# Summing the third and fourth kilocolumn of layer 0's modulation on VectorE during the gates and the merge, with a newly fitted order

## The chip, the cores and the metric

The kernel runs on one core of one Trainium2 chip. The metric is the time of one execution on the device in microseconds (us); shown is the median of several executions. The core's engines are TensorE (PE in the profile, with its weight loads as PEld), VectorE (DVE), ScalarE (ACT), GpSimd (POOL) and SyncE (SP), which issues nearly all DMAs here. Each engine runs its own instructions in the order in which the program lists them.

## What is computed

Two layers of a hybrid transformer over 256 latent and 256 context tokens of width 1024, all in float32. The part that the change touches is the modulation: a vector of 6144 numbers for each of the two conditioning vectors, six "kilocolumns" of 1024.

```python
s_c, s_cc = silu(c), silu(c_ctx)
for l in range(2):
    sh_m, sc_m, g_m, sh_f, sc_f, g_f = split(s_c @ w_mod[l] + b_mod[l], 6)         # latent tokens
    csh_m, csc_m, cg_m, csh_f, csc_f, cg_f = split(s_cc @ w_mod[l] + b_mod[l], 6)  # context tokens
    h = rmsnorm(x, norm_mix_g[l]) * (1 + sc_m) + sh_m
    y = merge(latent_attention(h), hyena(h), diff_attention(h))   # three branches, sigmoid gates, w_out
    x = x + g_m * y
    x = x + g_f * sqrelu_mlp(rmsnorm(x, norm_ffn_g[l]) * (1 + sc_f) + sh_f)
return rmsnorm(x, final_norm_g)
```

Kilocolumns 2 (`g_m`) and 3 (`sh_f`) of layer 0 are the "third and fourth". The first is needed at the residual that follows the output projection, the second at the norm before the feed-forward part.

## The kernel before

The work is a list of steps, `prog`, that the planner builds layer by layer (`layer`) and that the table `ORDER` permutes. `runner` walks through that list: it issues the weight loads on SyncE's queue as soon as a buffer of the ring is due, splits each weight piece ("unit") one unit ahead into a high part `whi` and a low part `wlo`, and calls the step. The table `CHOICE` says for single operations which engine takes them (A, D, P) or which PSUM bank ("m" is the bank `mod`). Below this the framework's scheduler sets the final order of each engine's instructions: it may pull a matmul forward into a place where it expects TensorE to wait.

A GEMM unit is 24 matmuls of 128x512 (lines 279, 280, 281: high times high, high times low and low times high over eight contraction tiles). Its weights come in a raw tile of 1 MB for two units, of which the ring holds two (`RAW_BUFS`); ScalarE makes `whi` (L231), VectorE or GpSimd `wlo` (L219), and there are three pairs of them (`UNIT_BUFS`).

Layer 0 runs in this order: input projections and latent attention (up to some 200 us), Hyena's long convolution and differential attention (to 300 us), gates and merge (300 to 451 us: 20 of the 24 gate units and eight branch steps), the output projection, then the feed-forward part (500 to 860 us). Layer 1 follows.

Layer 0's modulation is computed in two ways. Kilocolumns 0 and 1 are done at the start. Kilocolumns 2 to 5 are done on TensorE by `mod_group(0, 1)` and `mod_group(0, 2)`: eight steps each, and each step loads 1 MB of `w_mod` into the weight ring and issues four matmuls (L347) that write the four quarters of one PSUM bank. The weights are 32 columns wide (`spad`), so each matmul uses a quarter of the array's columns. A last step transposes the sums (L357) and adds the bias on VectorE. These 18 steps are woven into the attention steps.

Layer 1's modulation is done in another way, by `mod_cols`, during layer 0's feed-forward part: VectorE multiplies a loaded block `modr` by one number for each partition and adds it to one of two accumulators `macc` (L383; for the first block ScalarE does it, L381). When all eight blocks are in, four matmuls with a tile of ones sum over the partitions (`sums`, L397), and four transposes and two additions finish (`fin`, L406, L411).

Of the kernel before, what the change touches and what calls it, by code (L numbers as in the profile page):

```python
# [9 lines left out]
F32 = mybir.dt.float32  # L10
# [114 lines left out]
def backbone_kernel(ctx: ExitStack, tc: tile.TileContext, t, out):  # L125
# [5 lines left out]
    EG, TAIL, PT, PU, FD = (4, 14), 6, 4, 3, 2  # L131
    MQB, FB = 5, ("mod", "o")
# [34 lines left out]
    def bank2(tag, key):  # L167
        if "1" in key.split(".")[0][:2] and pick("bk" + tag + key, "-") == "m":
            return bank("mod", 1)
        return bank(tag)  # L170
# [198 lines left out]
    def mod_cols(l, c):  # L369
# [4 lines left out]
        def part(kt):  # L374
            def f(raw):
                if kt == 0:
                    box["acc"] = [S["ffn"].tile([128, 1024], F32, tag=f"macc{v}", name=f"macc{v}") for v in range(2)]
                for v, a in enumerate(box["acc"]):
                    sv = spad[:, kt, v:v + 1]
                    if kt == 0:  # L380
                        ACT.activation(out=a, in_=raw, func=AF.Copy, scale=sv)  # L381
                    else:
                        DVE.scalar_tensor_tensor(out=a, in0=raw, scalar=sv, in1=a, op0=ALU.mult, op1=ALU.add)  # L383
            return f
        for kt in range(KT):
            def load(kt=kt):
                raw = S["ffn"].tile([128, 1024], F32, tag="modr", name="modr", bufs=RAW_BUFS)
                SP.dma_start(out=raw, in_=t["w_mod"][l, kt * 128:(kt + 1) * 128, c * 1024:(c + 1) * 1024])
                return raw
            steps.append(Step(part(kt), blk=Blk(load, "ffn")))  # L390
# [1093 lines left out]
    def norm_into(l, w):  # L1484

        def f(s):
# [3 lines left out]
            if (l, w) == (DEPTH - 1, 1):  # L1490
                hb["r"] = t2k()[:, :NL]
                ACT.copy(hb["r"], r)
            make_h(l, w, s, r, own=True)
        return f

    def layer(l):
        nt = T if l == 0 else NL
        p = []
# [185 lines left out]
```

## Time and profile before

| | us |
|---|---|
| median of 3 runs (1324.16 to 1326.61) | 1326.32 |
| profiled execution, whole | 1327.46 |
| its span, first to last instruction | 1325.7 |
| TensorE busy | 1281.5 (97%) |
| VectorE busy | 868.3 (66%) |
| ScalarE busy | 579.7 (44%) |
| GpSimd busy | 262.9 (20%) |

Times in views of the trace count from the span's start. Matmuls are pipelined: a row shows a matmul as longer than the step to the next one, so what a matmul costs is read from start to start. In the timeline a row `x8` stands for eight records that follow each other; a float32 matmul leaves two records, so `x8` is four matmuls. The granted clock is 1.00 of 2.4 GHz in all stretches that matter here.

### The profile page before, as it was taken

To read this page: it belongs to the slowest core of one execution; us is meant where nothing else is said; L and a number is where in the kernel's file an instruction comes from. 1 tells how busy PE (TensorE), PEld (TensorE's weight loads), DVE (VectorE), ACT (ScalarE), POOL (GpSimd) and SP (SyncE) were. 2 spreads that over 40 slices of the span, in tenths; PEclk is the share of its full clock that TensorE was granted. 3 is DMA by queue.
4 is the path that set the end of the run, shared out by engine and by line. 5 is a ranking of instruction groups with operands and counts; after the bars stand their busy time and mean duration, and the time that the engine had idled before them with its cause. 6 is when DMAs were issued, how large, how long until landed. Compare 5 with 4: busy or idle time off the path is not lost. (4 is left out here: it accounts for less than half of the span.)

```text
span 1325.7 us, 19880 instructions
## 1 busy us (share of the span) xinstructions
PE 1281.5 (97%) x7934; PEld 1077.5 (81%) x7934; DVE 868.3 (66%) x1426; ACT 579.7 (44%) x1027; POOL 262.9 (20%) x233
## 2 busy tenths in 40 slices
PE   5999999999999999999999999998999999999997
PEld 3566777678888798787787877996788999999997
DVE  4776746865243568987584875588768557876555
ACT  4454552664222334332432331364546755645343
POOL 3111032210002112220100112122133343240210
PEclk8899999999999999999999999998999999999999
DMA  9643234443332324655563543332124355555552
GB/s 283 166 160 106 77 123 133 149 138 95 95 96 95 120 72 130 220 178 167 177 207 114 185 153 123 120 104 80 49 81 124 120 175 187 159 188 189 174 183 94
DMA packets 159790, 185.21 MB, mean 140 GB/s; under 512 B 4880, under 2 KB 149233, under 8 KB 157650
## 3 DMA queue, kind: packets, MB, share of 16 engines
q1 hardware_dynamic: 158162, 182.27, 43.7%
q0 software_dynamic: 928, 1.54, 0.4%
q8 instruction: 62, 1.02, 0.3%
q14 instruction: 30, 0.25, 0.1%
q10 hardware_dynamic: 608, 0.14, 0.0%
HBM read 182.88 MB, written 1.05 MB: 139 GB/s over the span
## 5 line engine op out<-in xcount | busy, mean ns | idle before, releaser
L231 ACT CAST whi<-raw 128x1024 fp32r<-128x1024 f32 x197 | 206.7, 1051 | 429.8 <-PE g L280 201.5
L279 PE MATMUL g<-hhi,whi 128*128 128x512 f32 (+2 forms) x1040 | 354.3, 341 | 4.3 <-DVE d L1179 1.7
L281 PE MATMUL g<-hhi,wlo 128*128 128x512 f32 (+2 forms) x1040 | 352.3, 339 | 0.1
L280 PE MATMUL g<-hlo,whi 128*128 128x512 f32 (+2 forms) x1040 | 351.9, 339 | 0.5 <-DVE hlo L506 0.5
L219 POOL TENSOR_TENSOR wlo<-raw,whi 128x512 fp32r<-128x512 f32 x138 | 187.6, 1380 | 647.3 <-ACT whi L231 508.2
L219 DVE TENSOR_TENSOR wlo<-raw,whi 128x1024 fp32r<-128x1024 f32 x161 | 199.7, 1242 | 151.0 <-ACT whi L231 144.5
L279 PEld LDWEIGHTS g<-hhi,whi 128*128 128x128 f32 x1040 | 195.4, 188 | 36.2 <-issue 4.7
L280 PEld LDWEIGHTS g<-hlo,whi 128*128 128x128 f32 x1040 | 196.1, 189 | 23.5 <-DVE hlo L506 0.7
L281 PEld LDWEIGHTS g<-hhi,wlo 128*128 128x128 f32 x1040 | 196.0, 189 | 22.7 <-issue 0.3
L383 DVE SCALAR_TENSOR_TENSOR macc<-modr,spad,macc 128x1024 f32<-128x1024 f32 x84 | 111.9, 1364 | 8.2 <-DMA modr<-in_w_mod_dram 7.5
L1364 DVE SCALAR_TENSOR_TENSOR x<-s,modT,x 128x256 f32<-128x256 f32 x95 | 43.5, 480 | 72.0 <-PE s L281 72.0
L281 PE MATMUL s<-hid0h,wlo 128*128 128x512 f32 (+1 forms) x256 | 86.9, 339 | 0.0
L280 PE MATMUL s<-hid0l,whi 128*128 128x512 f32 (+1 forms) x256 | 86.8, 339 | 0.0
L279 PE MATMUL s<-hid0h,whi 128*128 128x512 f32 (+1 forms) x256 | 86.7, 339 | 0.0
L279 PE MATMUL s<-hid1h,whi 128*128 128x256 f32 (+1 forms) x224 | 72.8, 325 | 0.0
L281 PE MATMUL s<-hid1h,wlo 128*128 128x256 f32 (+1 forms) x224 | 72.4, 323 | 0.0
L280 PE MATMUL s<-hid1l,whi 128*128 128x256 f32 (+1 forms) x224 | 72.4, 323 | 0.0
L809 DVE TENSOR_REDUCE sm<-s 128x1 f32<-128x512 f32 (+1 forms) x75 | 51.1, 689 | 30.2 <-PE s L281 17.3
L279 PEld LDWEIGHTS s<-hid0h,whi 128*128 128x128 f32 x256 | 48.4, 189 | 8.2 <-issue 1.7
L281 PEld LDWEIGHTS s<-hid0h,wlo 128*128 128x128 f32 x256 | 48.1, 188 | 5.7
L280 PEld LDWEIGHTS s<-hid0l,whi 128*128 128x128 f32 x256 | 48.0, 187 | 5.8
L157 ACT ACTIVATE t<-s,sm 128x512 f32<-128x512 f32 (+1 forms) x67 | 40.8, 614 | 26.0 <-DVE sm L809 25.7
(470 smaller groups left out, 2414.2 us busy)
## 6 DMA issues: line engine op xcount, KB each, us to landing
raw<-in_w_fc_dram SPq DMA_DIRECT2D x64, 1024.0 KB, 5.4
raw<-in_w_in_dram SPq DMA_DIRECT2D x34, 1024.0 KB, 5.3
modr<-in_w_mod_dram SPq DMA_DIRECT2D x48, 512.0 KB, 4.1
raw<-in_w_mod_dram SPq DMA_DIRECT2D x16, 1024.0 KB, 5.0
mq<-in_w_mod_dram SPq DMA_DIRECT2D x16, 512.0 KB, 7.7
raw<-in_w_out_dram SPq DMA_DIRECT2D x8, 1024.0 KB, 5.1
raw<-in_w_in_dram SPq DMA_DIRECT2D x8, 512.0 KB, 3.8
raw<-in_w_br_a_dram SPq DMA_DIRECT2D x8, 512.0 KB, 3.5
```

The lines of the kernel that those rows point to most:

```text
L157: ins = ACT.activation(out=out, in_=in_, func=func, **kw).ins
L219: e.tensor_tensor(out=u.lo[:, a:a + w], in0=src[:, a:a + w], in1=u.hi[:, a:a + w].bitcast(F32), op=ALU.subtract)
L231: cp(f"hi{u.id}")(u.hi, src)
L279: PE.matmul(ps, lhsT=ah, rhs=bh, start=first and i == 0, stop=False)
L280: PE.matmul(ps, lhsT=ah, rhs=bl, start=False, stop=False)
L281: PE.matmul(ps, lhsT=al, rhs=bh, start=False, stop=last and i == n - 1)
L383: DVE.scalar_tensor_tensor(out=a, in0=raw, scalar=sv, in1=a, op0=ALU.mult, op1=ALU.add)
L809: DVE.tensor_reduce(out=sm[:, c0:c0 + nseg], in_=ps.rearrange("p (s k) -> p s k", s=nseg), axis=AX.X, op=ALU.max, negate=True)
L1364: DVE.scalar_tensor_tensor(out=x[:, n, c], in0=ps[:, c], scalar=modT[l][:, goff + n, s:s + 1], in1=x[:, n, c], op0=ALU.mult, op1=ALU.add)
```

## The change

Layer 0's kilocolumns 2 and 3 are no longer done by `mod_group(0, 1)` but by `mod_cols`, woven into the gates and branches of the merge, in a new pool `mo`. There the blocks are 512 columns wide instead of 1024, so each kilocolumn has 16 loads of 256 KB with two buffers, and each block takes two operations of 128x512 (one for each conditioning vector). One of these (`mc3.4.1.1`) is given to ScalarE and GpSimd. `mod_group(0, 2)` stays on TensorE and takes the places of both groups. `ORDER` has 591 places instead of 562; outside the stretch up to the merge it moves mainly the `mod_cols` steps of the feed-forward part by a place or two, swaps two steps of differential attention in layer 1, and moves a few units of the last feed-forward part. In `CHOICE` some 20 of 180 entries differ, among them three more banks "m" in layer 1's two attentions.

```diff
 ORDER = (
-    (0, 17), 18, 17, 20, 19, 21, 24, (22, 24), (25, 27), (30, 32), (27, 30), 34, (32, 34), 36, 35, (37, 41), 42, 41,
+    (0, 17), 18, 17, 20, 19, 21, 24, (22, 24), (25, 27), 31, 30, (27, 30), 34, (32, 34), 36, 35, (37, 41), 42, 41,
...
+    M0, M1, M2 = (2, 3), (), ()
...
-    def mod_cols(l, c):
+    def mod_cols(l, c, pool="ffn"):
...
+        w = 512 if pool == "mo" else 1024
-        def part(kt):
+        def part(kt, h):
             def f(raw):
...
                 for v, a in enumerate(box["acc"]):
                     sv = spad[:, kt, v:v + 1]
+                    a = a[:, h * w:(h + 1) * w]
                     if kt == 0:
                         ACT.activation(out=a, in_=raw, func=AF.Copy, scale=sv)
+                    elif w == 512 and pick(f"mc{c}.{kt}.{h}.{v}", "D") == "P":
+                        q = t2k()
+                        ACT.activation(out=q, in_=raw, func=AF.Copy, scale=sv)
+                        POOL.tensor_tensor(out=a, in0=a, in1=q, op=ALU.add)
                     else:
                         DVE.scalar_tensor_tensor(out=a, in0=raw, scalar=sv, in1=a, op0=ALU.mult, op1=ALU.add)
...
+    def spread_mods(l, cs, pool):
+        m = []
+        fin = None
+        for c in cs:
+            s = mod_cols(l, c, pool)
+            m += s[:FD] + ([fin] if fin else []) + s[FD:-1]
+            fin = s[-1]
+        return m + [fin]
...
-            mods = mod_group(0, 1) + mod_group(0, 2)
...
-            p += [close_pool("df1"), close_pool("df0"), open_pool("m", "left")]
-            p = p[:40] + weave(p[40:], mods)
+            p += [close_pool("df1"), close_pool("df0"), open_pool("m", "left"), open_pool("mo", "left")]
+            p = p[:40] + weave(p[40:-4], mod_group(0, 2)) + p[-4:]
...
+        if l == 0:
+            p = q + weave(p, spread_mods(0, M0, "mo"))
```

What this does to the engines' own order is shown at three places. The first is TensorE's queue in differential attention of layer 0 (scores `s<-d`, transposes `t<-ident`, values `o<-t`, a gate GEMM `g<-hhi`), before:

```order
L837 MATMUL t<-ident,t 128x128 x4
L347 MATMUL mod<-raw,spad 32x512
L1224 MATMUL s<-d_2348,d_2240 128x512
L347 MATMUL mod<-raw,spad 32x512 x4
L857 MATMUL o<-t,dvt 64x128
L347 MATMUL mod<-raw,spad 32x512 x3
L279 MATMUL g<-hhi,whi 128x512
```

and the last place of this kind that is left there, after:

```order
L863 MATMUL o<-t,dvt 64x128
L351 MATMUL mod<-raw,spad 32x512 x3
L1242 MATMUL s<-d_1831,d_1880 128x256 x2
L850 MATMUL t<-ident,t 128x128 x2
L1242 MATMUL s<-d_1831,d_1880 128x256 x2
```

Three runs of modulation matmuls stand within four other rows before, and nothing of the kind stands behind the one row that is left. Over the whole queue there are 19 such rows with 64 matmuls before, and 11 rows with 32 matmuls after.

The second place is TensorE's queue at the end of the merge, after: the last matmuls of branch 7 (`yc`), the sums of kilocolumn 3, and the start of branch 6 (`ya`). Before, branch 6 follows branch 7 directly.

```order
L284 MATMUL g<-ycl,whi 128x512
L285 MATMUL g<-ych,wlo 128x512
L410 MATMUL mod<-macc_3256,ones 32x512 x2
L410 MATMUL mod<-macc_3257,ones 32x512 x2
L283 MATMUL s<-yah,whi 128x512
L284 MATMUL s<-yal,whi 128x512
```

The sums stand between two branches and need the last parts of VectorE's accumulators. The third place is VectorE's queue in the merge, around branch 3 (`t<-t,s` and its like multiply a gate with a branch's result or add two; `ml` is the low part of a merged result, the first one here that of branch 2), before:

```order
L1336 TENSOR_TENSOR t<-t,s 128x512
L286 TENSOR_TENSOR ml<-g,mh 128x512
L1336 TENSOR_TENSOR s<-t,s 128x512
L1341 TENSOR_TENSOR t<-t,s 128x512
L1336 TENSOR_TENSOR g<-t,g 128x512
L1341 TENSOR_TENSOR g<-t,g 128x512
L286 TENSOR_TENSOR ml<-g,mh 128x512
```

and after:

```order
L1349 TENSOR_TENSOR t<-t,s 128x512
L394 SCALAR_TENSOR_TENSOR macc_3256<-modr,spad,macc_3256 128x512
L1349 TENSOR_TENSOR s<-t,s 128x512
L394 SCALAR_TENSOR_TENSOR macc_3257<-modr,spad,macc_3257 128x512
L1354 TENSOR_TENSOR t<-t,s 128x512
L1349 TENSOR_TENSOR g<-t,g 128x512
L223 TENSOR_TENSOR wlo<-raw,whi 128x1024
L1354 TENSOR_TENSOR g<-t,g 128x512
```

The accumulations now stand between the operations of a branch and between the weight splits.

## Rows read from the trace of the kernel before

**Rows 1.** Page, section 1: busy us (share of span), instructions, by engine.
```profile
PE 1281.5 (97%) x7934; PEld 1077.5 (81%) x7934; DVE 868.3 (66%) x1426; ACT 579.7 (44%) x1027; POOL 262.9 (20%) x233
```

**Rows 2.** Stretches: length, busy PE, PEld, DVE, ACT, POOL, clock, DMA share, GB/s.
```profile
220.00:260.00 40.00, 36.75 (x209) 24.89 (x204) 34.49 (x68) 24.03 (x56) 13.00 (x12) 1.00 0.49 159
260.00:300.00 40.00, 40.00 (x235) 28.57 (x236) 25.67 (x49) 26.47 (x57) 5.67 (x5) 1.00 0.41 132
300.00:445.00 145.00, 145.00 (x626) 117.28 (x625) 53.81 (x64) 42.70 (x57) 16.34 (x13) 1.00 0.31 95
500.00:820.00 320.00, 319.89 (x1463) 256.75 (x1464) 234.76 (x268) 104.99 (x138) 53.74 (x33) 1.00 0.52 167
...
900.00:960.00 60.00, 52.32 (x357) 42.67 (x357) 46.64 (x101) 30.47 (x68) 12.14 (x13) 0.94 0.25 71
```

**Rows 3.** Timeline of PE, one modulation step: start, us, line, operands, records.
```profile
193.69 0.39 PE L281 MATMUL g<-hhi,wlo 128*128 128x512 f32 x1
194.00 1.07 PE L347 MATMUL mod<-raw,spad 128*32 128x512 f32 x8
195.00 0.50 PE L279 MATMUL g<-hhi,whi 128*128 128x512 f32 x1
195.34 0.39 PE L280 MATMUL g<-hlo,whi 128*128 128x512 f32 x1
```

**Rows 4.** Timeline of PE, a single modulation matmul (two records).
```profile
120.02 1.04 PE L347 MATMUL mod<-raw,spad 128*32 128x512 f32 x2
120.99 0.50 PE L281 MATMUL s<-kh,ql 96*128 96x512 f32 x1
```

**Rows 5.** Timeline of PE, modulation steps that a wait of TensorE follows.
```profile
99.07 1.06 PE L347 MATMUL mod<-raw,spad 128*32 128x512 f32 x8
100.86 0.44 PE L279 MATMUL g<-qnh,wqh 128*96 128x512 f32 x1 [0.73 <-DVE kl L981]
...
247.47 1.92 PE L347 MATMUL mod<-raw,spad 128*32 128x512 f32 x16
250.29 0.50 PE L279 MATMUL g<-hhi,whi 128*128 128x512 f32 x1 [0.90 <-DVE d L1179]
```

**Rows 6.** Timeline of PE, three modulation runs in differential attention.
```profile
258.94 1.04 PE L347 MATMUL mod<-raw,spad 128*32 128x512 f32 x2
...
260.35 1.06 PE L347 MATMUL mod<-raw,spad 128*32 128x512 f32 x8
...
261.71 1.06 PE L347 MATMUL mod<-raw,spad 128*32 128x512 f32 x6
```

**Rows 7.** Timeline of PE, `sums` and `fin` of one kilocolumn of layer 1.
```profile
607.24 0.40 PE L281 MATMUL s<-hid0h,wlo 128*128 128x512 f32 x1
607.57 1.07 PE L397 MATMUL mod<-macc,ones 128*32 128x512 f32 x8
608.56 0.50 PE L279 MATMUL s<-hid0h,whi 128*128 128x512 f32 x1
...
614.27 0.60 PE L406 MATMUL t<-ident,t 128*128 128x128 f32 x4
614.62 0.48 PE L279 MATMUL s<-hid0h,whi 128*128 128x512 f32 x1
```

**Rows 8.** Line 383, all instructions: duration ns min/median/max, first and last start.
```profile
L383 DVE SCALAR_TENSOR_TENSOR macc<-modr,spad,macc x84: 1271/1279/2392, 509.3 to 804.3; 128x1024 f32<-128x1024 f32 x84
```

**Rows 9.** Waits, 300 to 445 us: engine and line, releaser, total us, times, longest.
```profile
ACT whi L231 <- PE g L280: 76.0, 20, 4.9
```

**Rows 10.** Waits of DVE, 500 to 820 us.
```profile
DVE macc L383 <- DMA modr<-in_w_mod_dram: 7.5, 8, 3.8
```

**Rows 11.** Timelines of DVE and of POOL, 786 to 792 us.
```profile
787.73 2.39 DVE L383 SCALAR_TENSOR_TENSOR macc<-modr,spad,macc 128x1024 f32<-128x1024 f32 x1
...
787.74 3.53 POOL L219 TENSOR_TENSOR wlo<-raw,whi 128x512 fp32r<-128x512 f32 x2 [20.36 <-ACT whi L231]
```

**Rows 12.** Page, section 6: DMA issues, count, KB each, median us to landing.
```profile
modr<-in_w_mod_dram SPq DMA_DIRECT2D x48, 512.0 KB, 4.1
```

More of the change, by code (lines that the diff above doesn't have):

```diff
@@ L167, in bank2 @@
     def bank2(tag, key):
-        if "1" in key.split(".")[0][:2] and pick("bk" + tag + key, "-") == "m":
+        if pick("bk" + tag + key, "-") == "m":
             return bank("mod", 1)
@@ L367, in mod_group @@
         return steps
-    def mod_cols(l, c):
+    def mod_cols(l, c, pool="ffn"):
         box = {}
         steps = []
-        def part(kt):
+        w = 512 if pool == "mo" else 1024
+        def part(kt, h):
             def f(raw):
-                if kt == 0:
-                    box["acc"] = [S["ffn"].tile([128, 1024], F32, tag=f"macc{v}", name=f"macc{v}") for v in range(2)]
+                if kt == h == 0:
+                    box["acc"] = [S[pool].tile([128, 1024], F32, tag=f"macc{v}", name=f"macc{v}") for v in range(2)]
                 for v, a in enumerate(box["acc"]):
                     sv = spad[:, kt, v:v + 1]
+                    a = a[:, h * w:(h + 1) * w]
                     if kt == 0:
                         ACT.activation(out=a, in_=raw, func=AF.Copy, scale=sv)
+                    elif w == 512 and pick(f"mc{c}.{kt}.{h}.{v}", "D") == "P":
+                        q = t2k()
+                        ACT.activation(out=q, in_=raw, func=AF.Copy, scale=sv)
+                        POOL.tensor_tensor(out=a, in0=a, in1=q, op=ALU.add)
                     else:
@@ L385, in mod_cols, with load @@
         for kt in range(KT):
[L386 to L390, printed above, removed]
+            for h in range(1024 // w):
+                def load(kt=kt, h=h):
+                    raw = S[pool].tile([128, w], F32, tag="modr", name="modr", bufs=RAW_BUFS)
+                    c0 = c * 1024 + h * w
+                    SP.dma_start(out=raw, in_=t["w_mod"][l, kt * 128:(kt + 1) * 128, c0:c0 + w])
+                    return raw
+                steps.append(Step(part(kt, h), blk=Blk(load, pool)))
         def sums():
@@ L1541, in layer @@
             g = EG[1]
+        q = p
+        p = []
         for n2 in range(4):
             p += gates[max(g, 6 * n2):6 * n2 + 6] + branches[2 * n2:2 * n2 + 2]
+        if l == 0:
+            p = q + weave(p, spread_mods(0, M0, "mo"))
+        else:
+            p = q + p
         p += [close_pool("y2")] + ([close_pool("hy")] if l else []) + [close_pool("y")]
@@ L1552, in layer @@
             p.append(open_pool("tl", "right"))
-        p += down_steps(l, nt, t["w_out"][l], 0, lambda: S["mm"], 16, "g", norm_into(l, 1), kept if l == 0 else None)
+        d = down_steps(l, nt, t["w_out"][l], 0, lambda: S["mm"], 16, "g", norm_into(l, 1), kept if l == 0 else None)
         if l == 0:
-            p.append(close_pool("tl"))
+            p += (weave(d, spread_mods(0, M1, "mo")) if M1 else d) + [close_pool("tl"), close_pool("mo")]
+        else:
+            p += d
         p += [close_pool("m"), close_pool("ge"), open_pool("ffn", "right")]
@@ L1558, in layer @@
         if l + 1 < DEPTH:
-            m = []
-            fin = None
-            for c in range(6):
-                s = mod_cols(1, c)
-                m += s[:FD] + ([fin] if fin else []) + s[FD:-1]
-                fin = s[-1]
-            m.append(fin)
+            m = (spread_mods(0, M2, "ffn") if M2 else []) + spread_mods(1, range(6), "ffn")
             f = weave(f[:-13], m) + f[-13:]
```

75 rows, old and new, of tables (CHOICE, ORDER) are left out of this document.

## The prediction

> **What bounds the kernel now.** I read the page's busy times first: TensorE is busy for 97% of the span and no other engine for more than 66% [rows 1]. The weight loads are busy for only 81%, so the next question is whether TensorE's 97% is real. The timeline answers it: in a GEMM the next matmul starts 0.23 us after the last, and where something else is put between two GEMM matmuls, the start of the next is late by just that [rows 3]. The stretches then show where this holds. In the gates and the merge (300 to 445 us) TensorE is busy for the whole of the 145 us, with VectorE at 53.81 and ScalarE at 42.70; in the feed-forward part it is busy for 319.89 of 320 us although VectorE has 234.76 us of work there, and this is the part in which VectorE already sums layer 1's modulation [rows 2]. It does not hold at 220 to 260 us, where TensorE is busy for 36.75 of 40 us and VectorE for 34.49, nor at 900 to 960 us. So a microsecond of TensorE's work is worth a microsecond in most places and nothing in a few, and the sum has to be made place by place.
>
> **The price of a pass.** Line 347's matmuls use a quarter of the array each, and four of them into four quarters run side by side: the four start at 194.00 and the next GEMM matmul starts at 195.00 [rows 3]. A single one, at 120.02, holds the next matmul up until 120.99 [rows 4]. So what counts is not matmuls but passes: a run of one to four costs the same. From the GEMM matmul ahead (193.69) to the one behind (195.00) are 1.31 us; less that matmul's own 0.23 this is 1.08, and the matmul behind takes 0.34 instead of 0.23 to the next one [rows 3]. A pass costs 1.19 us.
>
> **What leaves TensorE.** The queue of before has 19 runs; those of five and of eight are two passes each, so 21 passes. The queue of after has 11 runs, one of eight: 12 passes. Nine passes go, net. By place:
> - Two go where TensorE then waits anyway: the step at 99.07 is followed by 0.73 us of waiting for VectorE, and the double step at 247.47, of which one pass stays, by 0.90 us [rows 5]. Without the pass the wait is longer. I take 0 for both; at most they give 1.19 each.
> - Nine go where no wait follows: those at 120.02 and 194.00 [rows 3, 4], three alike at 173.56, 208.89 and 282.61, one of two at 219.14, and the three at 258.94, 260.35 and 261.71 [rows 6]. 9 x 1.19 = 10.7 us.
> - Two come. One makes a second pass beside the transposes of Hyena's input (201.6 us), with no wait near it: +1.19. The other stands ahead of scores for which TensorE waits, in the stretch of 36.75 busy in 40 us [rows 2]: 0 taken, at most +1.19.
>
> That is 10.7 - 1.2 = 9.5 us off.
>
> **What comes back on TensorE.** Each of the two kilocolumns needs `sums` and `fin`. In the feed-forward part the sums hold the GEMM up from 607.24 to 608.56, which is 1.32 - 0.23 + 0.11 = 1.20 us, and the four transposes with the step behind them take 614.62 - 614.27 = 0.35, with 0.1 for the switch 0.45 [rows 7]. Twice 1.65 is 3.3; the old group's own four transposes go, 0.45. Net +2.85, and TensorE is at 9.5 - 2.85 = 6.65 us less.
>
> **What the pass covered.** The three passes at 258.94 to 261.71 stand within 4 us in differential attention, between scores, transposes and values of one chain [rows 6]. ScalarE works for 26.47 and VectorE for 25.67 of the 40 us there, and just ahead VectorE for 34.49 of 40 [rows 2]. Taking 3.6 us of TensorE's work out of such a chain will uncover some waiting for the softmax. The nearest rows are the two places above where a wait does follow [rows 5], and those give nothing back; the places without a wait give all. I take half, +1.8, with bounds 0 and 3.6. The other open places have GEMM matmuls behind them, and I take nothing there. **Sum: 6.65 - 1.8 = 4.85 us off.**
>
> **VectorE and ScalarE in the merge.** Two columns are 32 blocks of 512 columns. Four of them (the first contraction tile) go to ScalarE; the other 28 make 56 operations, of which 55 stay on VectorE. At 1279 ns for 1024 columns [rows 8] and some more for two halves, 0.67 us each: 55 x 0.67 = 37 us. VectorE comes to 53.81 + 37 = 91 of 145 us, 63%, against 73% in the feed-forward part, where TensorE loses 0.11 us in 320 [rows 2]. Costed at nothing. The cover is the weight buffers: in the merge ScalarE's split waits for TensorE to release a buffer 20 times, 76.0 us in all [rows 9], so the splits run as far ahead as three buffers let them, which is two units of 24 x 0.23 = 5.5 us, 11 us less the splits' own time: some 9 us, an estimate. If that cover were gone, each late unit would cost TensorE its lateness.
>
> **The loads.** 32 loads of 256 KB go to SyncE's queue in the merge, and 8 loads of 1 MB leave the attention. That is 8.4 MB in 145 us, 58 GB/s on 95, still under the feed-forward part's 167 [rows 2]. A load waits on SyncE's queue until VectorE frees the block before last, and the weight loads queue behind it. In the feed-forward part the same queue has 48 such loads, of 4.1 us each [rows 12], and nothing is lost; here a raw weight tile has two units, 11 us, to arrive. Costed at nothing.
>
> **The rest of the fit.** The `mod_cols` steps moved by a place in the feed-forward part lie under a full TensorE: nothing. The bank choices in layer 1 touch the stretch at 900 to 960 us, where TensorE is idle for 60 - 52.32 = 7.7 us [rows 2]. More banks can shorten a wait for a bank, but not for a result. I take 0, bounds 2.5 either way.
>
> The profiled execution took 1327.46 us, 1.14 more than the median, and the difference is carried over: 1326.32 - 4.9 = **1321.4 us**.
>
> **The rivals.**
> - **The passes were filling.** The scheduler put modulation matmuls where it expected TensorE to wait. If the four passes from 258.94 to 282.61 covered waits (4 x 1.19 = 4.8 instead of 1.8: +3.0) and the new pass ahead of the scores is not covered (+1.19), 0.7 us is left: 1325.7. For it: 34.49 of 40 us of VectorE just ahead, and the two waits of [rows 5]. Against: TensorE is busy for all 40 us of 260 to 300, with gate GEMMs between the scores. Chance 0.20.
> - **GpSimd and VectorE hinder each other.** An accumulation that started with a GpSimd split beside it took 2.39 us against 1.28, and the two halves of the split 3.53 [rows 8, 11]. The merge has 16.34 us of GpSimd work in 13 operations [rows 2]; if 12 of them hold one operation of VectorE up by 1.1 each, 13 us come on top (104 of 145), and if a third of these stands ahead of a branch's multiplications, TensorE waits 4 x 1.1 = 4.4 for a bank: 1325.8. For it: these rows. Against: half of the 84 accumulations took no more than 1279 ns [rows 8], and the feed-forward part has 53.74 us of GpSimd work and a full TensorE. Chance 0.03. The Trainium skill (GPSIMD Engine Reference, 1. Specifications) says the same as a rule: GpSimd shares its SBUF interfaces with VectorE and contends with instructions that have two SBUF inputs, as each of the 55 has. The trace agrees with the 2.39 us; by this rule the change picks the worst kind of VectorE operation, and the time would be this rival's.
> - **Slower: VectorE waits for blocks in the middle of a branch.** The accumulations stand between a branch's multiplications, and VectorE takes them in order. With two buffers, a third block in a row can't land before 4.1 us [rows 12] after the first was freed, while the second takes 1.3: a wait of up to 2.8 us, as the longest of 3.8 us in the feed-forward part shows [rows 10]. Behind it wait the multiplications that free the two banks of `s`, and then the next branch on TensorE. If four of the eight branches meet it, 4 x 2.8 = 11 us: 1332. It decides from 0.6 us per branch on (8 x 0.6 = 4.85). Against: 7.5 us of such waits in 84 accumulations [rows 10], and a gate unit stands between most branches. Chance 0.08.
> - **The fit gives more.** The banks take a third of the 7.7 us idle at 900 to 960 us away: 2.5 more, 1318.9. Chance 0.10.
>
> **How the numbers follow.** The forecast has 0.59, for 1318.5 to 1323.7; the rivals 0.20, 0.03, 0.08 and 0.10. A difference under 0.2%, 2.65 us, can't be told from none. Faster by more: the forecast but for its upper end (0.56) and the better fit (0.10), 0.66. Within: the rest of the forecast, the filling and the hindering, 0.26. Slower: 0.08. The range takes in the filling rival and the better fit with both covered passes paying (1321.4 - 2.5 - 2.4 = 1316.5): 1316.5 to 1327.0. What is left out is the slow rival and as much again.
>
> **What would show it.** After: line 351 with 64 records instead of 128, and some 12 passes of 1.0 us; the start of the merge (first branch matmul) about 7 us earlier, its end about 4 to 5; VectorE near 91 us in the merge with TensorE still full. If the merge starts only 3 us earlier, the passes were filling. If TensorE shows gaps in the merge behind a multiplication of VectorE, the slow rival is right. A gap ahead of `sums` would say that the last parts come late. If the stretch from the norm at 500 us to the end changes its length by more than 1 us, the fit did something that I have costed at nothing.

## The result and the profile after

The median went from 1326.46 us (4 runs) to 1316.88 us (4 runs), a ratio of 0.9934 with an interval from 0.9920 to 0.9947. Run again later beside more runs of the kernel before, the changed kernel had 1319.06 us (6 runs) against 1325.89 us (23 runs): 0.9947, from 0.9927 to 0.9967. The change is worth some 7 to 10 us. The prediction was 1321.4 us, a gain of 4.9: the first four runs are 4.5 us below it, the repeat 2.3. The sign and the range held, the size was about half to seven tenths of what came.

The profiled execution has a span of 1313.0 us. Busy times from its page, to compare with [rows 1]:

```profile
PE 1271.4 (97%) x7890; PEld 1074.0 (82%) x7890; DVE 900.2 (69%) x1482; ACT 588.9 (45%) x1041; POOL 261.3 (20%) x233
```

TensorE has 10.1 us less work, VectorE 31.9 us more. The stretches of [rows 2], after (length, busy time of PE, PEld, DVE, ACT, POOL, granted clock, DMA share, GB/s):

```profile
220.00:260.00 40.00, 40.00 (x229) 29.97 (x228) 33.65 (x74) 26.09 (x61) 9.48 (x10) 1.00 0.28 84
260.00:300.00 40.00, 38.83 (x211) 29.64 (x211) 25.83 (x49) 28.70 (x60) 2.56 (x2) 1.00 0.26 80
300.00:445.00 145.00, 144.70 (x632) 114.94 (x631) 91.19 (x121) 45.97 (x60) 17.26 (x13) 1.00 0.47 145
500.00:820.00 320.00, 319.91 (x1440) 254.69 (x1439) 230.67 (x260) 102.76 (x134) 53.20 (x34) 1.00 0.51 166
...
900.00:960.00 60.00, 54.34 (x414) 44.57 (x414) 42.96 (x94) 34.39 (x78) 7.95 (x7) 1.00 0.20 58
```

In the merge VectorE is at 91.19 us, as forecast, and TensorE is still full. To see where the time went, five marks serve that both kernels have: the first matmul of Hyena's input projection (the first row with `g<-hhi,whi`, called the first mark here and the first gate matmul in the expectations), the first matmul of the output projection (the merge's end), the last one of that part, the last of layer 1's first projections, and the last row with `mod<-ones,t`, 0.2 us ahead of the last matmul of all. The second row of each list is no mark of the table: it is the first branch matmul, where the prediction put the start of the merge. Timeline of PE, before:

```profile
73.23 0.80 PE L279 MATMUL g<-hhi,whi 128*128 128x512 f32 x1
...
305.88 0.40 PE L279 MATMUL s<-yah,whi 128*128 128x512 f32 x1
...
450.88 0.39 PE L279 MATMUL g<-mh,whi 128*128 128x512 f32 x1
...
497.81 0.28 PE L281 MATMUL s<-mh,tll 128*128 128x256 f32 x1
...
896.66 0.28 PE L281 MATMUL t<-hhi,kvwl 128*128 128x256 f32 x1
...
1317.47 0.36 PE L1592 MATMUL mod<-ones,t 128*128 128x1 f32 x2
```

and after:

```profile
71.01 0.80 PE L283 MATMUL g<-hhi,whi 128*128 128x512 f32 x1
...
289.19 0.80 PE L283 MATMUL s<-yah,whi 128*128 128x512 f32 x1
...
444.46 0.48 PE L283 MATMUL g<-mh,whi 128*128 128x512 f32 x1
...
490.23 0.28 PE L285 MATMUL s<-mh,tll 128*128 128x256 f32 x1
...
888.99 0.28 PE L285 MATMUL t<-hhi,kvwl 128*128 128x256 f32 x1
...
1305.44 0.36 PE L1615 MATMUL mod<-ones,t 128*128 128x1 f32 x2
```

Each column of the table is the difference of two neighbouring marks, read in the same way from the timeline of every kernel of this study:

| kernel | start to first mark | to the merge's end | output projection | feed-forward of layer 0, first projections of layer 1 | rest of layer 1 |
|---|---|---|---|---|---|
| before | 73.23 | 377.65 | 46.93 | 398.85 | 420.81 |
| after | 71.01 | 373.45 | 45.77 | 398.76 | 416.45 |
| changed_again | 76.31 | 373.34 | 45.77 | 398.78 | 417.11 |
| few_sums | 73.75 | 373.31 | 45.90 | 398.78 | 417.36 |
| l1_old | 71.81 | 373.34 | 45.77 | 398.78 | 419.00 |
| l1_all | 73.55 | 377.61 | 46.91 | 398.84 | 416.93 |
| banks_start | 71.92 | 377.68 | 46.83 | 398.80 | 419.65 |
| no_g1 | 73.94 | 374.97 | 46.71 | 398.82 | 420.51 |
| no_g2 | 71.75 | 378.42 | 47.04 | 398.79 | 419.61 |
| m5 | 70.95 | 390.88 | 45.77 | 405.02 | 418.45 |
| change_unfit | 72.46 | 382.51 | 45.90 | 398.76 | 419.41 |
| fit_only | 73.73 | 384.18 | 47.04 | 398.83 | 416.84 |
| one_step | 71.41 | 373.14 | 45.90 | 398.79 | 417.89 |
| more_steps | 72.71 | 374.18 | 45.77 | 398.79 | 417.29 |

The three middle columns agree to 0.1 us in the two executions of one program (after, changed_again), so single profiles are compared there. The first column doesn't: 71.01 and 76.31 us are the same program. So the change gives 4.2 to 4.3 us up to the merge's end, 1.2 us in the output projection, 0.1 us in the feed-forward part, and 3.7 to 4.4 us in layer 1, where the two executions differ by 0.7 us and the profile of before is the slowest of its kind (420.81). With the means of the last column given below, 2.5 us, the four stretches add up to 8.0 us.

### The profile page after: what moved, and what is told of

Its sections match the earlier page's. It is cut to its first block, busy times and chain, and to the rows that moved or that the text cites. A ratio compares the mean times of both kernels' runs of the same rounds, so it can differ in the third digit from the quotient of the medians.

```text
span 1313.0 us, 19943 instructions
## 1 busy us (share of the span) xinstructions
PE 1271.4 (97%) x7890; PEld 1074.0 (82%) x7890; DVE 900.2 (69%) x1482; ACT 588.9 (45%) x1041; POOL 261.3 (20%) x233
## 4 chain that ended last, share of the span: by engine, by line
PE 82%; DVE 9%; ACT 4%; DMA 3%; issue 1%; POOL 1%; ACTq 0%; SPq 0%; DVEq 0%; POOLq 0%
PE g L283 15%; PE g L284 15%; PE g L285 15%; PE s L283 9%; PE s L284 9%; PE s L285 9%; PE o L863 2%; PE t L850 2%; ACT whi L235 1%; DMA raw<-in_w_in_dram 1%; DVE wlo L223 1%; DVE macc L394 1%; ACT t L161 1%; DMA mq<-in_w_mod_dram 1%; DVE hlo L502 1%
## 5 line engine op out<-in xcount | busy, mean ns | idle before, releaser
L394 DVE SCALAR_TENSOR_TENSOR macc<-modr,spad,macc 128x1024 f32<-128x1024 f32 (+1 forms) x139 | 155.1, 1149 | 37.7 <-DMA modr<-in_w_mod_dram 28.7
```

## The experiments

**The changed kernel again**, with no edit:

> The changed kernel itself once more, beside the others. Layer 0's part as both traces show it behind the first gate matmul (5.4 us) and layer 1's part as the fit alone gave it (about 1.3 us) make 6.7: about 1319.7 us. If the first four runs stood for it, it is 1317 (9.5 us faster).

Measured: 1319.06 us, 0.9947 (0.9927 to 0.9967), nearer to the first of the two values, with an interval that holds both. The rows in the last section show what differed in the 5.3 us by which its first mark came later.

**Layer 1's part of the fit alone, and all but it.** In l1_all the kernel before gets these entries (and the changed kernel's order at four places of layer 1); in l1_old the changed kernel gets the opposite:

```diff
-    "hi141": "P", "hi242": "D", "v1.3": "D",
+    "hi242": "P", "rbm1.3": "D", "sq32": "D", "trd1.0.1": "D",
+    "bks1d5.0": "m", "bks1m0.0": "m", "bks1m0.1": "m",
```

> The kernel before with only layer 1's part of the new fit (nine entries of CHOICE, four places of ORDER); layer 0 stays as it was. Theory A, the fit of layer 1 is worth what the two traces show behind the feed-forward part (4.4 us: 1.8 at 900 to 930 us, where TensorE's clock no longer falls, 2.6 later): 3 to 4.5 us faster than before, and layer 0's marks (start of the merge, first matmul of the feed-forward part) where they were. Theory B, the clock falls or not by chance and the rest is small: less than 1.5 us faster on the median, and the profile may or may not show the clock fall at 917 us.

> The changed kernel with layer 1's choices and order as before, so that only layer 0's part of the change is left. Theory A: 5 to 5.5 us faster than before (the prediction's 4.85 and the 1.2 us between the merge and the feed-forward part), and from the first matmul of layer 1 to the end as long as before. Theory B: 8 to 9.5 us faster, like the changed kernel.

Measured: l1_all 1325.12 us, 0.9994 (0.9985 to 1.0003); l1_old 1320.26 us, 0.9954 (0.9941 to 0.9966). By the medians layer 1's part is worth 1.3 us alone, with an interval from 0.4 us slower to 2.0 us faster. The profiles say more, as eight of the table's profiles have the new part and six the old one (banks_start has two of its nine entries and is counted as old): the last column is 416.45 to 418.45 us (mean 417.29) with the new part, and 419.00 to 420.81 (mean 419.83) with the old. The two groups don't overlap. 2.5 us is what the profiles give, 1.3 the medians. In l1_all the median alone is within theory B's 1.5 us, but its profile and l1_old's 6.1 us lie between the two theories. Part of the 2.5 is the clock of which the next experiment speaks: it falls there in five of the eight (not in after, l1_all and fit_only) and in all of the six. Where it falls alike, to 0.66 in one stretch of 5 us and back to 1.00 in the next, the four new ones have a mean of 417.41 us (changed_again, few_sums, one_step, more_steps) and the two old ones 419.31 (l1_old, no_g2): 1.9 us.

**Two banks and one copy alone:**

```diff
+    "xe0.0": "A",
+    "bks1m0.0": "m", "bks1m0.1": "m",
```

> The kernel before with three entries alone: the bank of the first two scores of latent attention in layer 1 (bks1m0.0, bks1m0.1), and the engine of the first copy of the input (xe0.0, ScalarE). The two act at places that can be read apart. Theory A: the banks keep the clock up at 917 us, 1.8 us from 900 to 930; the copy gives the 2.2 us that the start is shorter by, so that the first gate matmul of 73.2 us comes at 71: 3.5 to 4 us faster together. Theory B: the start differs from run to run by that much, and the clock falls by chance: within 1.5 us of before.

Measured: 1324.86 us, 0.9991 (0.9980 to 1.0003). The banks don't keep the clock up, and the copy does not decide the start: nine profiles with `xe0.0` on ScalarE have the first mark at 70.95 to 76.31 us (mean 72.6), five without at 71.75 to 73.94 (mean 73.0). Theory A falls in both points: in banks_start the granted clock falls to 0.69 and 0.62 (913.24 to 918.24 and on to 923.24 us) around two waits of layer 1's attention. In the kernel before it falls there too, and the 1.00 that is given above for all stretches that matter does not hold here (stretches as above):

```profile
915.00:920.00 5.00, 3.06 (x15) 2.31 (x16) 4.54 (x14) 0.96 (x2) 0.94 (x1) 0.71 0.04 11
920.00:925.00 5.00, 5.00 (x20) 4.04 (x18) 3.55 (x7) 2.24 (x6) 0.00 (x0) 0.61 0.00 0
```

and its matmuls then step by 0.43 us instead of 0.23, the step at the lower of the clock's two levels, 1.2 GHz (timeline of PE; another wait, of 2.46 us, ends at 915.55):

```profile
918.92 0.80 PE L279 MATMUL s<-kh,qh 96*128 96x512 f32 x1 [1.34 <-ACT qh L803]
...
919.94 0.63 PE L281 MATMUL s<-kh,ql 96*128 96x512 f32 x1
920.37 0.63 PE L279 MATMUL g<-cnh,wkh 128*128 128x512 f32 x1
```

After, the same two waits are there (2.46 and 1.40 us) and the clock stays at 1.00; but changed_again, the same program, has 0.81 and 0.85 at 910 to 920 us. So part of the 4.4 us that one pair of traces shows in layer 1 is a matter of the execution.

**VectorE's accumulations left out.** Of VectorE's 55 accumulations of layer 0 the 8 of the last contraction tile stay, and the one that GpSimd has:

```diff
-                    else:
+                    elif w == 1024:
+                        DVE.scalar_tensor_tensor(out=a, in0=raw, scalar=sv, in1=a, op0=ALU.mult, op1=ALU.add)
+                    elif kt == KT - 1:
                         DVE.scalar_tensor_tensor(out=a, in0=raw, scalar=sv, in1=a, op0=ALU.mult, op1=ALU.add)
```

> The changed kernel with 48 of the 56 accumulations of layer 0 left out (all but the last contraction tile; loads, sums and the rest stay), so VectorE has some 31 us less in the merge. The prediction's theory, that the accumulations are covered: the same time as the changed kernel within 1 us, and the merge as long. The rival, that VectorE delays TensorE in the merge or behind it: 2 us or more faster than the changed kernel, and it shows between the start of the merge and the feed-forward part.

Measured: 1320.80 us, 0.9952 (0.9939 to 0.9965), no faster than with them, and the merge ends 373.31 us behind the first mark, against 373.34 to 373.45. The accumulations cost TensorE nothing. They do wait for their blocks, as the slow rival said; the changed kernel's waits at 300 to 445 us (engine and line, releaser, total us, times, longest):

```profile
DVE macc L394 <- DMA modr<-in_w_mod_dram: 19.4, 11, 4.4
```

and for TensorE at 290 to 445 us all that is left:

```profile
PE g L283 <- DVE ml L290: 0.3, 1, 0.3
```

**One group of passes left out of the kernel before.** The steps of a group but its first issue no matmuls (no_g1; in no_g2 the condition has `g == 2`):

```diff
                 for j in range(4):
-                    PE.matmul(box["ps"][32 * j:32 * j + 32, :], lhsT=spad[:, kt, :],
-                              rhs=raw[:, 512 * j:512 * (j + 1)], start=kt == 0, stop=kt == KT - 1)
+                    if l == 0 and g == 1:
+                        if kt == 0:
+                            PE.matmul(box["ps"][32 * j:32 * j + 32, :], lhsT=spad[:, kt, :],
+                                      rhs=raw[:, 512 * j:512 * (j + 1)], start=True, stop=True)
+                    else:
...
```

> The kernel before with the matmuls of the third and fourth kilocolumn's steps left out but for the first step (28 of 32 matmuls; loads stay). Nine passes go, from 99 to 195 us. The prediction's prices: nothing for 99.07, 0.8 for 104.95 (a wait of 0.4 follows), 1.19 for the seven others: 9.1 us from the first gate matmul to the transposes of Hyena's input (200.7 us). The filling rival: less than 6.

> The kernel before with the same left out for the fifth and sixth kilocolumn: the passes from 208 to 283 us go, where most of the waits are. The prediction's prices, from 200 us to the first branch matmul of the merge (305.9): 1.19 for 208.89, 2.4 for the two at 219.14, nothing for 222.25 (a wait for GpSimd follows), nothing to 1.2 for the two at 247.47, 3.6 less 1.8 uncovered for the three from 258.94 on, 1.19 for 282.61: 6.6 to 7.8 us. The filling rival, that those from 258.94 on cover waits: under 4.8.

Measured: 1323.51 us for no_g1, 0.9984 (0.9972 to 0.9997), and 1325.02 us for no_g2, 0.9997 (0.9985 to 1.0009). Without nine passes of group 1 the transposes of Hyena's input come 4.4 us earlier (122.99 us behind the first mark, 127.42 before), not 9.1, and at the merge's end 2.7 us are left. Without those of group 2 the merge ends 0.8 us *later*. This is the plainest miss of my price by place: passes that had no wait behind them covered one all the same. In no_g1 (timeline of PE) the transposes and scores that followed a pass now wait themselves:

```profile
106.49 0.66 PE L842 MATMUL t<-ident,t 128*128 128x128 f32 x4 [1.49 <-ACT t L157]
...
113.15 0.39 PE L279 MATMUL s<-kh,qh 96*128 96x256 f32 x1 [1.03 <-ACT t L157]
```

and in no_g2 the waits are as long as the passes and the waits behind them had been (1.95 us for 2.05, 2.99 for 2.82), with the clock at its lower level for much of the time behind them (timeline of PE, then stretches):

```profile
223.37 1.01 PE L1150 MATMUL g<-invt,ysp 128*128 128x128 f32 x3 [1.95 <-POOL ysp L1139]
...
250.06 0.80 PE L279 MATMUL g<-hhi,whi 128*128 128x512 f32 x1 [2.99 <-DVE d L1184]
```

```profile
220.00:230.00 10.00, 7.95 (x37) 7.23 (x38) 4.96 (x9) 1.15 (x3) 4.46 (x4) 0.66 0.65 220
...
250.00:260.00 10.00, 9.94 (x42) 7.25 (x43) 6.03 (x18) 5.29 (x17) 2.46 (x4) 0.70 0.26 92
```

Where the two passes of 219.14 had stood without a wait, TensorE now waits for VectorE too, 0.88 us at 217.53 and 1.47 at 220.10.

Before and after, the granted clock is 1.00 in all of 220 to 260 us. So what these runs fail to gain is in part the clock. The 30 records of Hyena's inverse transform that stand behind the wait for `ysp` take 6.15 us in no_g2 and 5.24 in no_g1 (granted clock 0.66 and 0.83 at 220 to 230 us), and 3.62 before and after: 2.5 and 1.6 us, about what no_g1 loses of its 4.4 again. The wait's length alone does not decide it, as no_g2 and no_g1 wait for 1.95 and 1.98 us there and the changed kernel for 1.92 at 1.00.

**The change without its fit, and the fit without the change.** change_unfit is the changed kernel in which all steps but the modulation's stand in the old order, with the old choices; fit_only is the kernel before with the new order of those steps and the new choices:

```diff
-    (0, 17), 18, 17, 20, 19, 21, 24, (22, 24), (25, 27), 31, 30, (27, 30), 34, (32, 34), 36, 35, (37, 41), 42, 41,
+    (0, 17), 18, 17, 20, 19, 21, 24, (22, 24), (25, 27), (30, 32), (27, 30), 34, (32, 34), 36, 35, (37, 41), 42, 41,
...
-    "lo15": "D",
+    "lo13": "D",
```

> The change without the fit: the changed kernel's steps for the modulation, at the changed kernel's places, but all other steps in the order of the kernel before, with its choices (layer 1 with them). Measured from the first gate matmul to the last matmul, since what lies ahead of it differs from run to run. Theory P, twelve passes instead of twenty-one pay by themselves: the merge ends 3.5 to 4.5 us earlier than before, as in the changed kernel (4.2). Theory F, passes taken away only uncover waits (the two runs that left a group out gained 2.7 us and lost 0.8 by the merge's end), and the new order of the other steps brings the rest: 0 to 2 us earlier.

> The fit without the change: the kernel before with both groups of modulation steps on TensorE at their old places, and all other steps and choices as in the changed kernel. Theory P: the end of the merge within 1 us of before, a gain of 1 to 2 us behind it (layer 1). Theory F: the end of the merge 2 us or more earlier than before.

Measured: 1329.73 us, 1.0031 (1.0020 to 1.0041), and 1331.75 us, 1.0047 (1.0034 to 1.0060). Both are slower than before; their merges end 4.9 and 6.5 us later, and neither theory had that. So the gain in layer 0 belongs to neither half alone. One place where the order decides is Hyena's inverse transform. In both kernels GpSimd splits a weight unit directly ahead of the product `ysp` that TensorE waits for. In change_unfit the split comes late, as ScalarE gets the unit's weights only at 218.59 us, and the product, whose input from VectorE is ready at 218.8 us, has to wait for the split's end (timelines of ACT, POOL and PE):

```profile
218.59 1.04 ACT L232 CAST whi<-raw 128x1024 fp32r<-128x1024 f32 x1 [7.39 <-DMA raw<-in_w_in_dram]
...
219.71 2.93 POOL L220 TENSOR_TENSOR wlo<-raw,whi 128x512 fp32r<-128x512 f32 x2 [6.48 <-ACT whi L232]
222.60 1.25 POOL L1144 TENSOR_TENSOR ysp<-ysp,t 128x512 f32<-128x512 f32 x1
```

```profile
223.91 6.28 PE L1155 MATMUL g<-invt,ysp 128*128 128x128 f32 x30 [3.97 <-POOL ysp L1144]
```

and after, the weights are there at 214.56 us, the split is over when the product's input is ready, and the wait is half as long:

```profile
214.56 1.04 ACT L235 CAST whi<-raw 128x1024 fp32r<-128x1024 f32 x1 [5.95 <-DMA raw<-in_w_in_dram]
...
215.74 2.50 POOL L223 TENSOR_TENSOR wlo<-raw,whi 128x512 fp32r<-128x512 f32 x2 [10.11 <-ACT whi L235]
218.20 1.26 POOL L1147 TENSOR_TENSOR ysp<-ysp,t 128x512 f32<-128x512 f32 x1
```

```profile
219.51 3.62 PE L1158 MATMUL g<-invt,ysp 128*128 128x128 f32 x30 [1.92 <-POOL ysp L1147]
```

The same 30 records then take 6.28 us instead of 3.62, as the clock falls in change_unfit too (stretches):

```profile
220.00:230.00 10.00, 6.09 (x30) 6.09 (x30) 2.40 (x5) 1.83 (x5) 4.04 (x4) 0.66 0.31 105
...
250.00:260.00 10.00, 7.38 (x37) 5.78 (x38) 6.24 (x18) 5.05 (x15) 2.96 (x4) 0.83 0.36 106
```

In fit_only these 30 records take 3.62 us and the clock falls less, to 0.95 and 0.88 at 230 to 250 us; where its 6.5 us are lost, and which of the other moves bring the changed kernel's gain, was not taken apart.

**No modulation step on TensorE at all:**

```diff
-    M0, M1, M2 = (2, 3), (), ()
+    M0, M1, M2 = (2, 3, 4), (), (5,)
...
-            p = p[:40] + weave(p[40:-4], mod_group(0, 2)) + p[-4:]
```

> The changed kernel carried on: no modulation step is left on TensorE. Kilocolumn 4 is summed in the merge too, kilocolumn 5 in the feed-forward part, the other steps in the changed kernel's order. The prices of the prediction: 12 passes go, five of them with no wait near (6.0 us), the other seven beside waits (0 to 4 us); two more sums and fins come, less the group's fin (2.9 us): 3 to 7 us faster than the changed kernel, if VectorE's 109 of 145 us in the merge stay covered. The rival, that VectorE no longer keeps up (in the merge with 18 us more, or at the norm that needs kilocolumn 4): no faster than the changed kernel, with waits of TensorE for VectorE between 290 and 500 us.

Measured: 1344.24 us, 1.0133 (1.0117 to 1.0149). Twelve more passes go, and the merge ends 17.4 us later than in the changed kernel. The first branch matmul stands 224.5 us behind the first mark instead of 218.2, so some 6 us of this are lost ahead of the merge, where now nothing stands in the waits (the longest is in the first row below; the granted clock falls to 0.74 at 200 to 210 us and 0.66 at 220 to 230). 11 are lost in the merge, which has a third column's sums and `fin`, where the sums wait for VectorE's accumulators for 2.7 us in all (second row; timeline of PE) and gate matmuls for its `ml` for 3.2, with a clock of 0.66 at 345 to 350 us. 6 more go in the feed-forward part:

```profile
199.81 0.55 PE L285 MATMUL g<-whi,hhi 128*128 128x256 f32 x1 [3.79 <-DVE d L1194]
...
345.14 2.58 PE L412 MATMUL mod<-macc,ones 128*32 128x512 f32 x6 [2.08 <-DVE macc L396]
```

The order of these steps was not fitted, so neither the size nor the sign is shown to be the idea's own; the run shows that in this order twelve passes fewer bring the first branch matmul 6 us later.

**Passes moved into waits.** one_step moves one modulation step of the changed kernel forward past four others (the expectation says six places), more_steps all eight:

```diff
-    (43, 50), 52, (50, 52), (53, 60), 62, 65, 63, (60, 62), 64,
+    (43, 50), 52, (50, 52), (53, 58), 63, (58, 60), 62, 65, (60, 62), 64,
```

> The changed kernel with one modulation step moved six places forward, so that its four matmuls stand in TensorE's wait for VectorE's kl (96.50 to 98.63 us), where none stands now, instead of a run of one at 100.16 with no wait near. If passes are worth what the place says (nothing in a wait of 1.9 us, 1.0 to 1.2 in the open): the merge ends 1.0 to 1.5 us earlier than in the changed kernel, that is 5.2 to 5.7 earlier than before. If the waits behind grow by as much: no earlier.

> The changed kernel with all eight modulation steps moved forward, the first as above; eleven passes, and none is left behind 217 us, where the changed kernel has two (223.06 and 240.45). By the worth of places: three passes less in the open, 2 to 2.5 us earlier at the merge's end than the changed kernel. If passes from 217 to 260 us keep TensorE's clock up, as the runs without them suggest (granted clock 0.66 and 0.70 there): a fall of the clock between 217 and 260 us, and no gain.

Measured: 1317.47 us, 0.9939 (0.9926 to 0.9952), and 1318.93 us, 0.9953 (0.9941 to 0.9966): neither can be told from the changed kernel. The merge ends 0.2 us earlier and 0.8 us later than there. In one_step the four matmuls do stand in the wait, and the wait shrinks from 1.73 us to 0.73; but the next step now waits for its weights, whose ring has two buffers (timeline of PE):

```profile
97.22 1.07 PE L350 MATMUL mod<-raw,spad 128*32 128x512 f32 x8
99.02 0.44 PE L282 MATMUL g<-qnh,wqh 128*96 128x512 f32 x1 [0.73 <-DVE kl L993]
...
103.32 1.05 PE L350 MATMUL mod<-raw,spad 128*32 128x512 f32 x2 [0.85 <-DMA raw<-in_w_mod_dram]
```

The clock did not fall in more_steps, so what I expected of it for that reason is wrong too.

## Why the prediction was right, and where it was not

- **Bound and place.** Right: TensorE is the bound, and VectorE's 37 more us in the merge cost it nothing. few_sums shows the cover: 47 accumulations fewer move the merge's end by 0.1 us.
- **Passes.** 21 became 12, as counted. By the timeline the runs of line 347 last 24.7 us from first start to the next matmul, and those of line 351 13.9, 10.8 us less. That is not to be held against my 9.5, as it leaves out the switch and takes in the waits behind the runs, 3.8 us before and 1.8 after; without these it is 8.8 us, 0.98 for each of nine passes, and with the switch as I priced it (0.2) my 10.7 for nine. (The 0.23 us between GEMM matmuls in my price is not in [rows 3]; the timeline has it, as at 306.12, 306.35 and 306.58 us before.) A run of three matmuls costs 0.99 us, one of eight in a place with a wait 2.55:

```profile
134.20 1.06 PE L351 MATMUL mod<-raw,spad 128*32 128x512 f32 x6
135.19 0.51 PE L283 MATMUL s<-kh,qh 96*128 96x512 f32 x1
...
195.94 1.92 PE L351 MATMUL mod<-raw,spad 128*32 128x512 f32 x16
198.49 0.35 PE L283 MATMUL g<-whi,hhi 128*128 128x256 f32 x1 [0.62 <-DVE d L1192]
```

- **Sums and fins.** Forecast 3.3 us. From first start to the next matmul they take 0.99 + 1.00 for the sums and 0.90 + 0.36 for the fins, 3.25; counted as in the forecast, with the switch (0.2 for a sum, 0.1 for a fin), 3.85. The sums and one fin cost what I said; the other fin, of 0.90, has a wait for `ml` behind it, which makes the 0.55 us more:

```profile
374.78 0.60 PE L419 MATMUL t<-ident,t 128*128 128x128 f32 x4
375.68 0.50 PE L283 MATMUL g<-hhi,whi 128*128 128x512 f32 x1 [0.30 <-DVE ml L290]
...
437.40 1.06 PE L410 MATMUL mod<-macc,ones 128*32 128x512 f32 x8
438.39 0.50 PE L283 MATMUL s<-yah,whi 128*128 128x512 f32 x1
```

- **What the passes covered: the sum came out, the reason did not hold.** I let nine passes pay in full but for 1.8 us, and got 4.85 for a part that measures 4.2 to 4.3. But that step assumed that a pass with no wait behind it covers nothing, that the clock stays where it is without the passes, and that the other steps' order only follows. no_g1, no_g2 and change_unfit refute this: with the old order, passes taken out give half of their time, nothing, or a loss, as waits come up and the clock falls behind some of them. My filling rival had the waits right for the bare change, though not the clock, and I gave it 0.20 because TensorE was busy for all of 260 to 300 us. A busy TensorE is no evidence there: the pass itself is what makes it busy. That the fitted order then gives 4.2 us is near to my sum by luck as much as by its terms.
- **The start of the merge.** I had the first branch matmul about 7 us earlier. Behind the first mark it is 14.5 us earlier (218.18 us, 232.65 before). The order explains part of it: of the 24-matmul units whose rows read `g<-hhi,whi` and its like, seven stand between 150 us behind the first mark and the first branch, eight before, and one such unit is 24 x 0.23 = 5.5 us. Some 9 us are left, where I had 7. The merge is then 10.2 us longer (155.27 us, 145.00 before), that unit and the sums and fins in the main. So this sign can't tell the forecast from the filling rival without the order being counted off.
- **Behind the merge.** The output projection is 1.2 us shorter; I had no term for it. Before, it waits for `ml` (timeline of PE):

```profile
455.08 0.40 PE L279 MATMUL g<-mh,whi 128*128 128x512 f32 x1
456.30 0.50 PE L280 MATMUL g<-ml,whi 128*128 128x512 f32 x1 [0.83 <-DVE ml L286]
```

After, there is no such wait. change_unfit has the shorter part too (45.90 us) and fit_only not (47.04), so it goes with the change and not with the fit. That the last sums and fin give VectorE the time for `ml` fits this, but was not tested.
- **The rest of the fit.** The mis-sized term. I took 0 with 2.5 us either way, since more banks shorten no wait for a result. Layer 1's part of the fit is worth 2.5 us by the profiles (1.9 where the clock falls alike) and 1.3 by the medians. That is at the upper bound I gave. A wait of 0.54 us for VectorE's `d` (L1179) at 980.8 us is one piece that is gone; the long waits at 900 to 920 us are not gone, as I had said. The rival that the fit gives more had 0.10; with its 2.5 us and the output projection's 1.2 the sum would have been 1317.7.
- **The other rivals.** The slow one had its condition, longer than I had it (blocks late 11 times, up to 4.4 us against 2.8), and not its effect. The splits do run ahead, as I had it: ScalarE's wait for TensorE to free a buffer is 68.6 us in all at 300 to 445 us, 76.0 before; that this is the reason no run tested. GpSimd did hinder VectorE: three accumulations started while an operation of GpSimd was under way and took 1.79, 1.78 and 1.50 us against 0.746; the two others that met one had started ahead of it and took 0.75 and 0.74 (line 394, duration min/median/max):

```profile
L394 DVE SCALAR_TENSOR_TENSOR macc<-modr,spad,macc x55: 739/746/1785, 297.5 to 427.0; 128x512 f32<-128x512 f32 x55
```

No other of the 55 took over 0.8 us, and TensorE lost nothing by it. The Trainium skill's rule (GPSIMD Engine Reference, 1. Specifications), that GpSimd contends with VectorE's instructions of two SBUF inputs, is borne out by these three and decides nothing here.

## What to carry to other kernels

Work that fills an engine's waits can't be priced by looking for a wait behind it: take it out in one run and see what comes up, the granted clock included, before its time is counted as gain. A change that takes filler out and a new order belong together: each alone was slower than before here, both together faster. Where a program's executions differ by more than an edit is worth, compare stretches between marks that both traces have, over several profiles.

## What was not expected of the hardware

Two executions of the changed kernel differ by 5.3 us ahead of the first mark and by 0.1 us in the 373 us behind it. The granted clock differs: at 45 to 55 us it was 1.00 in one (first row) and 0.60 in the other (second row), with 59 and 40 matmul records. TensorE's waits differ too, 9.5 and 13.1 us in all from 10 to 77 us; which of the two brought the other about is not shown.

```profile
45.00:55.00 10.00, 9.60 (x59) 5.15 (x60) 9.31 (x23) 4.58 (x10) 0.96 (x1) 1.00 0.81 226
```

```profile
45.00:55.00 10.00, 9.45 (x40) 4.03 (x40) 6.78 (x18) 2.27 (x5) 0.64 (x1) 0.60 0.68 179
```

The other place is around the two waits of layer 1's attention, in stretches of 5 us: down to 0.61 in the profile of before and to 0.81 in changed_again, 1.00 after, with the same waits of 2.46 and 1.3 to 1.4 us. These are the two places where executions of one program were seen to differ; the kernel before alone ranges from 1322.4 to 1330.5 us.
